# One computed order for all engines of a two-layer hybrid decoder trunk, with up products that keep tokens stationary and later transposes done by VectorE and DMAs

## The chip, the cores and the metric

The kernel runs on one core of one Trainium2 chip. The metric is the device time of one launch in microseconds (us); the figure used for a kernel is the median over its runs. Inside the core five engines run side by side: PE (TensorE, matmuls), DVE (VectorE), ACT (ScalarE), POOL (GpSimd) and SP (SyncE, which here only issues DMAs).

## What is computed

A trunk of two layers on 256 tokens of width 2048, all in float32. Layer 0 mixes tokens with a causal softmax attention of 16 heads and a forget gate ("fox"), layer 1 with three dilated window groups of 8 heads ("dil"). A squared-ReLU MLP of width 8192 follows each mixer.

```python
D_MODEL = 2048; SEQ = 256; DEPTH = 2; HEAD_DIM = 128; D_FF = 8192

def rms_norm(x, g):
    y = x * lax.rsqrt(jnp.mean(x * x, axis=-1, keepdims=True) + EPS)
    return y * g

def sq_relu_mlp(h, w_up, w_down):
    a = jax.nn.relu(h @ w_up)
    return (a * a) @ w_down

def reference(x, ...):
    for i in range(DEPTH):
        h = rms_norm(x, mix_norm_g[i])
        mix = fox_attention(h, ...) if i == 0 else dilated_attention(h, ...)
        x = x + mix                      # each mixer ends in o @ w_out
        h = rms_norm(x, mlp_norm_g[i])
        x = x + sq_relu_mlp(h, mlp_w_up[i], mlp_w_down[i])
    return x
```

In both attentions q and k are normed per head (`rms_norm(q, q_gain)`), and the mixers' input products are `h @ w_in`.

## The kernel before

**Products.** Float32 accuracy is had from fp32r matmuls: each operand is split into a high part (fp32r) and the rest, and a product is three matmuls, high*high + high*rest + rest*high. Weights come from HBM in pieces of 256 rows x 512 columns (`load`, L272, 512 KB, five buffers), and `split` cuts each on ACT (L288, `wh`, the high part) and DVE (L289, `wl`, the rest), five buffers each. A piece serves two steps k of 128 rows. `product` (L317 to L319) keeps the tokens of `hT` (or `aTh`/`aTl`, `oT`) as the stationary operand and streams 512 weight columns: for each k and each half of the tokens three matmuls of 512 columns into one PSUM bank. All mixers' input products, both output projections and the MLP's down products go this way.

**Up products.** `product_transposed` (L365, L369) keeps the weights stationary, so that the result comes out with channels on partitions, as the down product needs it. For each k and each of four blocks of 128 channels, one matmul streams the high and the rest parts of the 256 tokens side by side (512 columns, L365) and one streams the high part against the weights' rest (256 columns, L369). `up_chain` adds the two halves of each bank (ACT L842, DVE L843), squares (DVE L848) and splits (ACT L851, DVE L852) into `aTh` and `aTl`. The down product multiplies by the squared inverse norm at its end (`add_chain`, L805).

**Transposes.** Tokens with channels on partitions (`hT`) are made by `norm_chain`. For the first norm (`n0`) and for the last quarter of the three later ones PE transposes (L434, four 128x128 blocks at a time), since the next stage waits for these; the other quarters are turned by `transposed_by_dma`: DVE turns 32x32 blocks (L399), four DMAs write them to DRAM (L402), one reads them back (L404). Queries and keys go the same way in `qk_chain` (with the reading DMA on POOL's queue, L534), except two products (`by_engine`), which PE transposes (L506).

**Heads.** A head's work on PE is a group of score matmuls (L704, L610, L613), three transposes of the probabilities (`p_transposed`, L584) and the weighted values (`pv`, L576 and L577), with DVE and ACT between them.

**What sets the order.** The program writes instructions in one order and a scheduler places them; `Jobs` lets chains wait a fixed number of ticks (one tick is one k of a product) between their steps. `issue_after` holds some instructions behind others. Each engine runs its own instructions in order. At the start SP loads the first half of the first token block, half a weight piece (the other half goes by ACT's queue) and the second half of the block, and `wake` (L117) runs dummy transposes. `last_product` (L343 to L345) ends the kernel in three parts so that stores overlap.

Of the kernel before, what the change touches and what calls it, by code (L numbers as in the profile page):

```python
# [17 lines left out]
P = 128  # L18
# [5 lines left out]
KC = D // P  # L24
DFF = 4 * D
# [9 lines left out]
RAW_BUFS = 5  # L35
W_BUFS = 5
W_SUB = 2
RAW_SUB = 2


class Jobs:

    def __init__(self):
        self.now = 0
        self.live = []
        self.done = set()  # L50
        self.running = False

    def spawn(self, gen):
        self.live.append([self.now, None, gen])
        if not self.running:
            self._run()

    def _run(self):
        self.running = True
        for job in list(self.live):  # L60
            while job[0] <= self.now and (job[1] is None or job[1] in self.done):
                try:
                    got = next(job[2])
                except StopIteration:
                    self.live.remove(job)
                    break
                if isinstance(got, int):
                    job[0], job[1] = self.now + got, None
                    if not got:
                        continue  # L70
                else:
                    job[1] = got
        self.running = False

    def tick(self):
        self.now += 1
        self._run()

    def need(self, key):
        tries = 0  # L80
        while key not in self.done:
            self.tick()
            tries += 1
            assert tries < 10000, key
# [3 lines left out]
def trunk(ctx: ExitStack, tc, x, fox_w_in, fox_b_f, fox_q_gain, fox_k_gain, fox_w_out, dil_w_in,  # L88
          dil_q_gain, dil_k_gain, dil_w_out, mix_norm_g, mlp_norm_g, mlp_w_up, mlp_w_down, out):
    nc = tc.nc  # L90
    jobs = Jobs()

    const = ctx.enter_context(tc.tile_pool(name="const", bufs=1))
    act = ctx.enter_context(tc.tile_pool(name="act", bufs=1))
    wpool = ctx.enter_context(tc.tile_pool(name="wpool", bufs=1))
    work = ctx.enter_context(tc.tile_pool(name="work", bufs=1))
    small = ctx.enter_context(tc.tile_pool(name="small", bufs=8))
    dram = ctx.enter_context(tc.tile_pool(name="dram", bufs=1, space=bass.MemoryType.DRAM))
    ps_acc = ctx.enter_context(tc.tile_pool(name="ps_acc", bufs=4, space=PSUM))
    ps_tp = ctx.enter_context(tc.tile_pool(name="ps_tp", bufs=2, space=PSUM))  # L100
    ps_sc = ctx.enter_context(tc.tile_pool(name="ps_sc", bufs=2, space=PSUM))


    warm = small.tile([P, 1], F32, tag="warm", name="warm", bufs=1)
    nc.gpsimd.memset(warm, 0.0)
    nc.scalar.activation(warm, warm, AF.Exp)
    ident = const.tile([P, P], F32, name="ident")
    make_identity(nc, ident)
    mhalf = const.tile([P, 8], F32, name="mhalf")
    nc.gpsimd.memset(mhalf, -0.5)  # L110


    spare = ps_sc.tile([P, P], F32, tag="sc", name="spare")

    def wake(times):
        for _ in range(times):
            nc.tensor.transpose(spare, ident, ident)  # L117

    wake(8)


    gain = const.tile([P, 4 * KC + 8], F32, name="gain")
    MLP_G, FOX_G, DIL_G = 2 * KC, 4 * KC, 4 * KC + 2

    def gain_rows(name, sources):
        rows = work.tile([2 * KC, P], F32, tag="s", name=name, bufs=4)
        at = 0
        for src in sources:
            nc.sync.dma_start(rows[at:at + src.shape[0], :], src)
            at += src.shape[0]  # L130
        return rows[0:at, :]

    def gain_columns(name, rows, at):
        n = rows.shape[0]
        ps = ps_tp.tile([P, 512], F32, tag="tp", name=f"ps_{name}")
        nc.tensor.transpose(ps[:, :n], rows, ident[:n, :n])
        return nc.vector.tensor_copy(gain[:, at:at + n], ps[:, :n])

    per_chunk = "l (c p) -> (l c) p"
    mix_rows = gain_rows("g_mix", [mix_norm_g.rearrange(per_chunk, p=P)])  # L140


# [848 lines left out]
```

## Time and profile before

| What | us |
|---|---|
| median of 3 runs (lowest, highest) | 2164.76 (2164.07, 2165.49) |
| span of the profiled execution, first to last instruction | 2163.6 |
| PE busy | 2153.5 |
| DVE busy | 1395.5 |
| ACT busy | 1108.1 |
| POOL busy | 70.8 |
| DMA moved | 454.11 MB, 210 GB/s over the span |

The time of the profiled execution itself is not listed apart from its span; the median of the runs lies 1.2 us above that span. "Busy" of PE counts overlapping matmuls, so it says that PE has work, not how fast it goes; the pace is read from the distance between starts. Nearly the whole span PE is busy, at full granted clock in every slice, while DVE is busy for 64% and ACT for 51% of it.

### The profile page before, as it was taken

Reading aid. Unit: us, or ns where it says so; the run is one execution under the profiler, and the core shown is the slowest. Engines: PE = TensorE matmul, PEld = TensorE weight load, DVE = VectorE, ACT = ScalarE, POOL = GpSimd, SP = SyncE. Lnnn points to the kernel's source line nnn. Section 1 sums busy time; section 2 is a strip of 40 time slices with the busy share of each in tenths; the row PEclk is TensorE's granted clock in tenths of the full one; section 3 lists DMA queues with packets and bytes.
Section 4 is the critical chain, followed back from the end, with each engine's and each line's share of the span. In section 5 each row is a group of like instructions: output and inputs, shape, how many; then the busy total and the mean of one; then the engine's idle time right before and its main releaser. Section 6 shows DMA issues by size and latency. Waiting matters only on the chain.

```text
span 2163.6 us, 30020 instructions
## 1 busy us (share of the span) xinstructions
PE 2153.5 (100%) x11251; PEld 1918.3 (89%) x11251; DVE 1395.5 (64%) x1847; ACT 1108.1 (51%) x1536; POOL 70.8 (3%) x87
## 2 busy tenths in 40 slices
PE   9999999999999999999999999999999999999999
PEld 8888888998998998998888888888988988988988
DVE  6777796665665565566667777766655655655664
ACT  6655655544444454455555555655544543544542
POOL 1111000000000000000010010000000000000000
PEclk9999999999999999999999999999999999999999
DMA  8676658666666766767776776767666666666764
GB/s 253 219 224 190 222 175 264 200 202 202 201 203 203 200 201 204 203 199 242 216 251 204 242 224 198 240 203 237 203 204 201 199 204 204 200 202 203 203 211 140
DMA packets 285683, 454.11 MB, mean 210 GB/s; under 512 B 21144, under 2 KB 99040, under 8 KB 285536
## 3 DMA queue, kind: packets, MB, share of 16 engines
q1 hardware_dynamic: 282240, 442.36, 65.7%
q0 software_dynamic: 2880, 9.44, 1.2%
q8 instruction: 88, 1.44, 0.3%
q10 hardware_dynamic: 416, 0.39, 0.1%
q14 instruction: 59, 0.48, 0.1%
HBM read 435.86 MB, written 16.25 MB: 209 GB/s over the span
## 4 chain that ended last, share of the span: by engine, by line
PE 95%; DVE 2%; ACT 1%; DMA 1%; issue 1%; POOL 0%; SPq 0%; ACTq 0%; DVEq 0%; POOLq 0%
PE acc L318 20%; PE acc L319 20%; PE acc L317 20%; PE up_n3a_acc L365 5%; PE up_n1a_acc L365 5%; PE up_n3a_tp L365 3%; PE up_n3a_sc L365 3%; PE up_n1a_tp L365 3%; PE up_n1a_sc L365 3%; PE up_n1a_acc L369 3%; PE up_n3a_acc L369 3%; PE up_n1a_sc L369 1%; PE up_n3a_sc L369 1%; PE up_n1a_tp L369 1%; PE up_n3a_tp L369 1%; DVE wl L289 1%
## 5 line engine op out<-in xcount | busy, mean ns | idle before, releaser
L289 DVE TENSOR_TENSOR wl<-raw,wh 128x1024 fp32r<-128x1024 f32 x799 | 974.8, 1223 | 692.2 <-ACT wh L288 690.1
L288 ACT CAST wh<-raw 128x1024 fp32r<-128x1024 f32 x799 | 837.2, 1048 | 924.1 <-PE acc L319 591.7
L317 PE MATMUL acc<-wh,hT_n 128*128 128x512 f32 x896 | 344.4, 385 | 0.0
L318 PE MATMUL acc<-wl,hT_n 128*128 128x512 f32 x896 | 340.1, 380 | 0.1
L319 PE MATMUL acc<-wh,hT_n 128*128 128x512 f32 x896 | 340.0, 380 | 0.0
L317 PE MATMUL acc<-wh,aTh_n1a 128*128 128x512 f32 x512 | 194.0, 379 | 0.0
L318 PE MATMUL acc<-wl,aTh_n1a 128*128 128x512 f32 x512 | 194.0, 379 | 0.0
L319 PE MATMUL acc<-wh,aTl_n1a 128*128 128x512 f32 x512 | 194.0, 379 | 0.0
L319 PEld LDWEIGHTS acc<-wh,hT_n 128*128 128x128 f32 x896 | 169.6, 189 | 24.1
L317 PEld LDWEIGHTS acc<-wh,hT_n 128*128 128x128 f32 x896 | 170.0, 190 | 22.6 <-ACT hT_n L440 0.7
L318 PEld LDWEIGHTS acc<-wl,hT_n 128*128 128x128 f32 x896 | 169.9, 190 | 22.3 <-DVE wl L289 0.5
L317 PE MATMUL acc<-wh,aTh_n3a 128*128 128x512 f32 x480 | 181.9, 379 | 0.0
L318 PE MATMUL acc<-wl,aTh_n3a 128*128 128x512 f32 x480 | 181.9, 379 | 0.0
L319 PE MATMUL acc<-wh,aTl_n3a 128*128 128x512 f32 x480 | 181.9, 379 | 0.0
L365 PE MATMUL up_n1a_acc<-hT_n,wh 128*128 128x512 f32 x512 | 181.6, 382 | 0.0
L365 PE MATMUL up_n3a_acc<-hT_n,wh 128*128 128x512 f32 x512 | 181.6, 382 | 0.0
L369 PE MATMUL up_n1a_acc<-hT_n,wl 128*128 128x256 f32 x512 | 139.6, 273 | 0.0
L369 PE MATMUL up_n3a_acc<-hT_n,wl 128*128 128x256 f32 x512 | 139.6, 273 | 0.0
L318 PEld LDWEIGHTS acc<-wl,aTh_n1a 128*128 128x128 f32 x512 | 96.8, 189 | 13.8
L319 PEld LDWEIGHTS acc<-wh,aTl_n1a 128*128 128x128 f32 x512 | 96.8, 189 | 13.7
L317 PEld LDWEIGHTS acc<-wh,aTh_n1a 128*128 128x128 f32 x512 | 96.8, 189 | 13.6
L365 PEld LDWEIGHTS up_n1a_acc<-hT_n,wh 128*128 128x128 f32 x512 | 96.8, 189 | 13.5
(730 smaller groups left out, 3209.4 us busy)
## 6 DMA issues: line engine op xcount, KB each, us to landing
raw<-in_mlp_w_up_dram SPq DMA_DIRECT2D x256, 512.0 KB, 4.0
raw<-in_mlp_w_down_dram SPq DMA_DIRECT2D x256, 512.0 KB, 3.7
raw<-in_dil_w_in_dram SPq DMA_DIRECT2D x192, 256.0 KB, 3.2
raw<-in_fox_w_in_dram SPq DMA_DIRECT2D x95, 512.0 KB, 4.1
raw<-in_fox_w_out_dram SPq DMA_DIRECT2D x32, 512.0 KB, 3.9
raw<-in_dil_w_in_dram SPq DMA_DIRECT2D x32, 512.0 KB, 6.6
raw<-in_dil_w_out_dram SPq DMA_DIRECT2D x32, 512.0 KB, 4.5
blocks_n<-turned_n SPq DMA_DIRECT2D x72, 64.0 KB, 1.9
```

The source lines that it names most:

```text
L288: issued["cast"] = nc.scalar.copy(hi, raw)
L289: issued["cut"] = nc.vector.tensor_sub(lo, raw, hi.bitcast(F32))
L317: nc.tensor.matmul(acc[t], ah[:, tok], hi, start=first, stop=False)
L318: nc.tensor.matmul(acc[t], ah[:, tok], lo, start=False, stop=False)
L319: issued["product"] = nc.tensor.matmul(acc[t], al[:, tok], hi, start=False, stop=last)
L365: issued["product"] = nc.tensor.matmul(banks[b], hi[:, i, col], in_turn(tokens.rearrange("p x s -> p (x s)"), P // 2), start=first, stop=last)
L369: nc.tensor.matmul(banks[b][:, 0:S], lo[:, i, col], in_turn(tokens[:, 0, :], P // 2), start=False, stop=False)
```

## The change

The file is rewritten around a planner. The program no longer issues instructions as it goes; it records operations with an engine, a written-down duration, and the buffers they read and write. `Plan.order` then runs all of them once through a model of five engines (PE, ACT, DVE, POOL, DMA), takes on each engine the ready operation that is due first, and issues everything in the resulting order, with no scheduler behind it. What else is different:

- Up products use the same form as all others (`Unit.whole`, L384 to L386): tokens stationary, 512 weight columns streaming. From the second period of 2048 hidden columns on, blocks of an up unit alternate with blocks of a down unit of the period before (`UU_D`); a block is one weight piece, 12 matmuls.
- The result then has tokens on partitions. ACT takes the ReLU, scaled by the inverse norm (L952), DVE turns 32x32 blocks (L995), four DMAs write 128 KB each to DRAM and one reads 512 KB back (`through_dram`, L444, L449, all on SP's queue), ACT squares (L1003), and ACT and DVE split (L1008, L1010). The squared inverse norm in the down product's end is gone (L523 adds only).
- All transposes after the first norm go through DVE and DRAM, the last quarter of each norm (`normed`) and the two products that PE transposed included; POOL issues no DMA any more. PE keeps the transposes of the first norm and of the probabilities.
- Six buffers for weight pieces and four for each split part, with one more of each in the MLP phases (`MORE`).
- Two products that follow a norm are paired: six blocks of one, six of the other, then two and two (`paired`).
- The first two fox products (queries and keys) go two blocks at a time in turn.
- `HALVED` is empty, so `quarters` and `parts` never run; the token sums for them (`sums_of_tokens`, 8 times) are still made, and no product reads them.

The core of it:

```diff
+    def run(self):
+        engines = ("pe", "act", "dve", "pool", "dma")
...
+                heapq.heappush(rows[what.eng], (not what.urgent, what.due, what.i, what))
...
+            op = heapq.heappop(rows[eng])[-1]
+            op.at = now
...
+        def whole(self, raw, keys, j, first, last):
+            hi, lo = cut(raw, keys, 0, 2 * NC, j in self.adding)
+            for i in range(2):
+                k = 2 * j + i
+                def go(k=k, i=i):
+                    h, l = (in_turn(r(w)[:, i * NC:(i + 1) * NC], NC // 2) for w in (hi, lo))
+                    for t in range(NT):
+                        acc = v(self.banks[t])
+                        a, b = (self.source.at(k, x, t) for x in range(2))
+                        nc.tensor.matmul(acc, a, h, start=first and i == 0, stop=False)
+                        nc.tensor.matmul(acc, a, l, start=False, stop=False)
+                        nc.tensor.matmul(acc, b, h, start=False, stop=last and i == 1)
+                plan.product(6 * 0.216, go, [hi, lo, *self.source.keys(k)], self.banks)
-                def main(first, last):
-                    issued["product"] = nc.tensor.matmul(
-                        banks[b], hi[:, i, col], in_turn(tokens.rearrange("p x s -> p (x s)"), P // 2), start=first, stop=last)
-                def rest():
-                    nc.tensor.matmul(banks[b][:, 0:S], lo[:, i, col], in_turn(tokens[:, 0, :], P // 2), start=False, stop=False)
+    def through_dram(turned, into, size=NT * NC):
+        blocks = blocks_ring.take()
+        for i in range(4):
+            def go(i=i):
+                nc.sync.dma_start(v(blocks)[:, :, :, i, :].rearrange("t j c x -> c t j x"),
+                                  v(turned)[32 * i:32 * i + 32, 0:size].rearrange("p (t j x) -> p t j x", t=NT, j=4))
+            add("dma", 0.45, go, reads=[turned], writes=[(blocks, i)])
+        def back():
+            nc.sync.dma_start(v(into)[:, 0:size].rearrange("p (t y) -> p t y", t=NT),
+                              v(blocks).rearrange("t j c i x -> (j c) t (i x)"))
+        add("dma", moved(512), back, reads=[(blocks, i) for i in range(4)], writes=[into])
+    def up_end(l, phase, source, halved):
...
+                        nc.scalar.activation(halves(v(z)[:, t * NC:(t + 1) * NC], S), by_column(v(banks[t]), S), AF.Relu, scale=by(t))
...
+            add("dve", 1.4, lambda: nc.vector.transpose(
...
+            through_dram(turned, z)
...
+    UU_D = "UUDUDUDUDUDUDUDD"
...
+                for u, d in zip(ups, downs):
+                    for c in UU_D:
+                        (u if c == "U" else d).block()
...
+    def paired(a, b, n=6):
+        a.blocks(n)
+        b.blocks(n)
+        a.blocks(NP - n)
+        b.blocks(NP - n)
...
-    by_engine = {("fk", 3), ("dqk", 3, 2)}
-    def wake(times):
-    wake(8)
+    add("pe", 1.0, lambda: wake(8), writes=["woken"], urgent=True)
```

Three places of the order follow. The first is PE in an up product. Before (`up_n1a` are PSUM banks, `wl`/`wh` the parts of the weights, here two blocks of 128 channels and the start of the next product):

```order
L369 MATMUL up_n1a_0_acc_3865<-hT_n_7_3919,wl_3970 128x256
L365 MATMUL up_n1a_0_acc_3865<-hT_n_7_3919,wh_3969 128x512
L369 MATMUL up_n1a_0_acc_3866<-hT_n_7_3919,wl_3970 128x256
L365 MATMUL up_n1a_0_acc_3866<-hT_n_7_3919,wh_3969 128x512
L365 MATMUL up_n1a_1_tp_4124<-hT_n_0_3408,wh_4009 128x512 [waits Activation_49]
```

and now, where an up block (`bank_A`, tokens `hT`) ends and a down block (`bank_E`, `aT`) begins:

```order
L384 MATMUL bank_A<-hi_128,hT_112 128x512
L385 MATMUL bank_A<-lo_132,hT_112 128x512
L386 MATMUL bank_A<-hi_128,hT_112 128x512
L384 MATMUL bank_E<-hi_129,aT_116 128x512
L385 MATMUL bank_E<-lo_133,aT_116 128x512
L386 MATMUL bank_E<-hi_129,aT_116 128x512
```

Pairs of 512 and 256 columns became triples of 512, and down work stands between up blocks.

The second is PE at the start of the program. Before (`x_103` is the first token block, its halves on two DMA lanes):

```order
L117 MATMUL spare<-ident 128x128 [waits Pool_49]
L117 MATMUL spare<-ident 128x128 x7
L136 MATMUL ps_g_mix<-ident,g_mix 128x32 [waits DMAHW1_49]
L117 MATMUL spare<-ident 128x128 x3
L434 MATMUL ptx_n_0_146<-ident,x_103 128x128 [waits DMAHW2_49]
L434 MATMUL ptx_n_0_146<-ident,x_103 128x128 x3
L117 MATMUL spare<-ident 128x128 x3
L317 MATMUL acc_0_190<-wh_142,hT_n_0_151 128x512 [waits Activation_49]
```

and now:

```order
L655 MATMUL bank_C<-ident 128x128 [waits Pool_49]
L655 MATMUL bank_C<-ident 128x128 x7
L697 MATMUL bank_E<-ident,x_68 128x128 [waits DMAHW0_49]
L697 MATMUL bank_E<-ident,x_68 128x128 x3
L666 MATMUL bank_E<-ident,fox_s_163 128x32 [waits DMAHW2_49]
L697 MATMUL bank_E<-ident,x_68 128x128 [waits DMAHW4_49,DVE_49,Activation_49]
L697 MATMUL bank_E<-ident,x_68 128x128 x3
L384 MATMUL bank_A<-hi_126,hT_112 128x512
```

The transposes of the block's second half moved ahead of the first product, and the dummy transposes between are gone.

The third is ACT after an up product. Before (`up_chain`):

```order
L288 CAST wh_7267<-raw_7265 128x1024 [waits DMAHW7_49,DVE_49,PE_49]
L842 COPY z_n1a_2_0_7293<-up_n1a_2_sc_7108 128x256 [waits PE_49]
L842 COPY z_n1a_2_0_7293<-up_n1a_2_sc_7109 128x256 [waits PE_49]
L842 COPY z_n1a_2_1_7298<-up_n1a_2_acc_7110 128x256 [waits PE_49]
L288 CAST wh_7289<-raw_7287 128x1024 [waits DMAHW0_49,DVE_49,PE_49]
L842 COPY z_n1a_2_1_7298<-up_n1a_2_acc_7111 128x256
L851 CAST aTh_n1a_4_7304<-z_n1a_2_0_7293 128x512 [waits DVE_49]
```

and now (`up_end`; `mlp_z` holds the ReLU and then the rows read back from DRAM):

```order
L340 CAST mlp_hi_2630<-raw_123 128x1024 [waits DMAHW3_49,DVE_49,PE_49]
L952 ACTIVATE mlp_z_2627<-bank_A,rstd_75 128x512 [waits PE_49]
L952 ACTIVATE mlp_z_2627<-bank_A,rstd_75 128x512
L340 CAST hi_126<-raw_124 128x1024 [waits DMAHW4_49,DVE_49]
L340 CAST hi_127<-raw_125 128x1024 [waits DMAHW5_49,DVE_49,PE_49]
L340 CAST hi_128<-raw_120 128x1024 [waits DMAHW6_49,DVE_49,PE_49]
L340 CAST hi_129<-raw_121 128x1024 [waits DMAHW7_49,DVE_49,PE_49]
L340 CAST mlp_hi_2630<-mlp_raw_2629 128x1024 [waits DMAHW0_49,DVE_49,PE_49]
L1003 ACTIVATE mlp_tr_2624<-mlp_z_2627 128x4x128 [waits DMAHW4_49,DMAHW5_49,DMAHW3_49,DMAHW6_49,DMAHW1_49,DVE_49]
L1003 ACTIVATE mlp_tr_2624<-mlp_z_2627 128x4x128 [waits Activation_49]
L340 CAST hi_126<-raw_122 128x1024 [waits DVE_49,PE_49]
```

ACT now waits for a DMA in the middle of its casts, five casts after the ReLU; the casts that follow are queued behind that wait.

More of the change, by code (lines that the diff above doesn't have):

```diff
@@ L33 @@
 N_SLOPES = 3 * DH
[L35 to L84, printed above, removed]
+PERIODS = DFF // D
@@ L105, in trunk @@
+    warm = T["sm31"]
     nc.gpsimd.memset(warm, 0.0)
     nc.scalar.activation(warm, warm, AF.Exp)
[L107 removed]
     make_identity(nc, ident)
[L109 to L113 removed]
+    nc.gpsimd.memset(T["mhalf"], -0.5)
     def wake(times):
         for _ in range(times):
[L117 to L122 removed]
@@ L123, in trunk @@
[L123 to L137, printed above, removed]
+            nc.tensor.transpose(T["C1"][:, 0:P], ident, ident)
```

1669 lines of the change are left out of this document (957 added, 712 removed).

## The prediction

> **What bounds the kernel now.** I read the page of the profile first, then the waits of PE.
>
> ```profile
> span 2163.6 us, 30020 instructions
> ...
> PE 2153.5 (100%) x11251; PEld 1918.3 (89%) x11251; DVE 1395.5 (64%) x1847; ACT 1108.1 (51%) x1536; POOL 70.8 (3%) x87
> ...
> PE 95%; DVE 2%; ACT 1%; DMA 1%; issue 1%; POOL 0%; SPq 0%; ACTq 0%; DVEq 0%; POOLq 0%
> ```
>
> ```profile
> PE po_f L576 <- DVE pTl_f L589: 2.2, 3, 0.7
> ...
> PE pc L674 <- DVE g_lf L671: 1.1, 1, 1.1
> ...
> PE sc_d L610 <- DVE sd L759: 0.2, 1, 0.2
> ```
>
> PE is without work for 2163.6 - 2153.5 = 10.1 us, and only 2.2 + 1.1 + 0.2 = 3.5 us of that are waits inside the stream (columns: total, times, longest); the rest lies at the two ends. The chain of work that ended last is PE for 95%. So an edit is worth what it takes out of PE's stream or puts into it, and work on the other engines costs nothing until PE waits for it. The next view says how far they are from that (groups by line: busy, mean ns, idle before and whom it ended with).
>
> ```profile
> L289 DVE TENSOR_TENSOR wl<-raw,wh 128x1024 fp32r<-128x1024 f32 x799 | 974.8, 1223 | 692.2 <-ACT wh L288 690.1
> L288 ACT CAST wh<-raw 128x1024 fp32r<-128x1024 f32 x799 | 837.2, 1048 | 924.1 <-PE acc L319 591.7 <-PE up_n1a_acc L365 150.1 <-PE up_n3a_acc L365 150.0
> ```
>
> ACT's casts of weights stand idle 892 us (591.7 + 150.1 + 150.0) because PE has not yet freed a buffer: the cuts are ahead of PE, not behind it.
>
> **Pace of PE: -7.3 us.** Busy time says nothing of pace, since matmuls overlap; starts do. The timeline of PE gives the first and last of two unbroken stretches (start, length).
>
> ```profile
> 358.79 0.38 PE L317 MATMUL acc<-wh,oTfh 128*128 128x512 f32 x1
> ...
> 381.24 0.38 PE L319 MATMUL acc<-wh,oTfl 128*128 128x512 f32 x1
> ```
>
> ```profile
> 449.91 0.38 PE L365 MATMUL up_n1a_acc<-hT_n,wh 128*128 128x512 f32 x1
> ...
> 465.95 0.38 PE L365 MATMUL up_n1a_acc<-hT_n,wh 128*128 128x512 f32 x1
> ```
>
> The first is 105 matmuls with tokens stationary, so 22.45 / 104 = 0.2159 us from start to start. The second is 50 pairs of an up product, 16.04 / 49 = 0.3274 us for 512 + 256 columns. The new form streams the same columns as 1.5 matmuls of 512: 1.5 x 0.2159 = 0.3238. There are 2048 pairs (32 up products x 16 k x 4 blocks of channels), so 2048 x 0.0036 = 7.3 us go. I take this as certain to within 1 us: the form that replaces it is the one measured beside it, with the same weight loads.
>
> The Trainium skill (TensorE: Matmul & The Clock Gate, section Back-to-back issue gap) gives N/2.4 + 2.5 ns for a gap between matmuls. For 512 columns that is 215.8 ns, and the trace agrees. For 256 it is 109.2 ns, where the trace leaves 327.4 - 215.9 = 111.5. By the rule this term would be 2048 x 1.25 ns = 2.6 us and the time some 5 us higher; the trace decides.
>
> **Transposes taken from PE: -4.3 us.** Four in an up product, in the same timeline, and their counts by line:
>
> ```profile
> 383.86 0.38 PE L365 MATMUL up_n1a_acc<-hT_n,wh 128*128 128x512 f32 x1
> 384.07 0.60 PE L434 MATMUL ptx_n<-ident,x 128*128 128x128 f32 x4
> 384.43 0.36 PE L369 MATMUL up_n1a_sc<-hT_n,wl 128*128 128x256 f32 x1
> 384.62 0.38 PE L365 MATMUL up_n1a_sc<-hT_n,wh 128*128 128x512 f32 x1
> ```
>
> ```profile
> L434 PE MATMUL ptx_n<-ident,x 128*128 128x128 f32 x56 | 9.4, 295 | 0.3 <-DMA x<-in_x_dram 0.3
> ```
>
> From L365 to L365 it is 0.76 us where 0.33 is usual: 0.43 for four. The code leaves 32 of the 56 (the first norm) and takes 24, and all 16 of L506: ten groups, 4.3 us. A late turn through DRAM could give some of it back; paired units put 12 blocks, 12 x 12 x 0.2159 = 31.1 us, ahead of the first product that needs the last quarter, and the turn has a price in the trace:
>
> ```profile
> L399 DVE STREAM_TRANSPOSE turned_n<-x 128x512 f32<-128x512 f32 x18 | 12.6, 700 | 0.0
> L842 ACT COPY z_n1a<-up_n1a_acc 128x256 f32<-128x256 f32 x32 | 11.8, 369 | 0.0
> L843 DVE TENSOR_TENSOR z_n1a<-up_n1a_acc,z_n1a 128x256 f32<-128x256 f32 x32 | 13.2, 414 | 0.0
> L848 DVE SCALAR_TENSOR_TENSOR z_n1a<-z_n1a 128x512 f32<-128x512 f32 x32 | 21.8, 680 | 0.0
> L851 ACT CAST aTh_n1a<-z_n1a 128x512 fp32r<-128x512 f32 x32 | 19.9, 623 | 4.4 <-DVE z_n1a L848 4.4
> ```
>
> ```profile
> raw<-in_mlp_w_up_dram SPq DMA_DIRECT2D x256, 512.0 KB, 4.0
> ...
> blocks_n<-turned_n SPq DMA_DIRECT2D x72, 64.0 KB, 1.9
> ```
>
> Turning 1024 columns is 2 x 0.70 on DVE, four writes that land in 1.9 us at half the new size (taken twice, 3.8), a read of 512 KB (4.0, as a weight piece) and a cast and a cut of 1.05 and 1.22: 11.5 us, some 15 with scaling and queues. That fits into 31.1 twice.
>
> **The up rows' new road: nothing.** Per up unit ACT had four L842 and two L851 (2.7 us) and now has two ReLUs and two squares (four of about 0.62, as L851) and a cast of 1.05: 3.5. DVE had four L843, two L848 and two of L852 like it (4.4) and now 1.40 + 1.22 = 2.6. With 16 pieces of 1.05 and 1.22 in the 41.4 us of an up and a down unit (32 steps of six matmuls), ACT comes to some 20 of 41.4 and DVE to 22. The road takes about 14 us by the same rows, 18 with queues; the blocks behind which its product stands are 13 in the interleaved periods, 33.7 us. ACT's wait for the read-back has five casts ahead of it, and what is queued behind it are casts, for which PE would wait only after it has used up those five, 5 x 2.59 = 13 us. If the cover were gone, each us of delay would be a us of the kernel. The token sums that nothing reads (8 times about 4 us on two engines) stay under the same cover.
>
> DMA: 32 x 1 MB more.
>
> ```profile
> 550.00:600.00 50.00, 50.00 (x308) 46.04 (x307) 30.67 (x36) 25.06 (x32) 0.00 (x0) 1.00 0.68 201
> ```
>
> The engines' share is 0.68 (before the GB/s). By bytes (1 MB on 8) it becomes 0.77; if each 512-byte packet cost as much as one of 2 KB, 1280 packets on 4096 make it 0.89. Neither bounds. On SP the writes and the read stand between weight loads that are six or seven pieces ahead.
>
> **Waits in the stream: -2.0 us.** The 3.5 us may vanish or grow. Before, the weighted values stand 12 products behind their transposes in 15 of 16 fox heads, and three of these waited 0.7 us. In the new order 12 of 16 stand 18 to 48 products behind, the dil heads 18 to 42, and the four at 12 have a score group between. Scores stand 138 products (29.8 us) or more behind their key unit; the same chain before:
>
> ```profile
> 130.50 0.69 ACT L484 ACTIVATE sq_('fk', 1)_0_1427<-acc,rstd_n 128x512 f32<-128x512 f32 x1
> ...
> 156.08 0.42 DVE L552 TENSOR_TENSOR fkT_1l<-sq_('fk', 1)_0_1427,fkT_1h 128x256 fp32r<-128x256 f32 x1
> ```
>
> 26 us. So I leave 1.5 us of waits. Bounds: none, or 0.7 at each of the 32 weighted products, 22.4 us.
>
> **Start: +1.0 us.** PE's first rows, and the stretches of the first 10 us (last two columns: DMA share, GB/s):
>
> ```profile
> 5.30 1.12 PE L434 MATMUL ptx_n<-ident,x 128*128 128x128 f32 x4 [0.32 <-DMA x<-in_x_dram]
> 6.21 0.85 PE L117 MATMUL spare<-ident 128*128 128x128 f32 x3
> 6.98 0.80 PE L317 MATMUL acc<-wh,hT_n 128*128 128x512 f32 x1
> ...
> 9.27 0.63 PE L319 MATMUL acc<-wh,hT_n 128*128 128x512 f32 x1
> 9.70 1.06 PE L434 MATMUL ptx_n<-ident,x 128*128 128x128 f32 x4
> 10.41 1.10 PE L317 MATMUL acc<-wh,hT_n 128*128 128x512 f32 x2
> ```
>
> ```profile
> 2.00:4.00 2.00, 2.00 (x9) 1.67 (x9) 0.43 (x1) 0.75 (x2) 1.84 (x4) 1.00 0.87 225
> 4.00:6.00 2.00, 1.68 (x8) 1.21 (x9) 0.94 (x9) 0.62 (x1) 0.50 (x2) 1.00 0.93 306
> ...
> 8.00:10.00 2.00, 2.00 (x7) 1.53 (x6) 1.16 (x2) 0.46 (x1) 0.00 (x0) 1.00 0.97 324
> ```
>
> Now the first product stands behind the second half of the token block, the fifth transfer on SP: 256 + 512 + 16 + 512 + 256 KB = 1.59 MB. At those rates 0.45 + 0.61 MB are in by 6.0, and the rest at 324 GB/s by 7.6. Four transposes take 0.91 there (5.30 to 6.21), so the first product starts near 8.6 instead of 6.98, 1.6 later, with a transpose group done that stood at 9.70 and took 0.71. Net 0.9, rounded to 1.0. The slow products at the beginning, 2.29 us for the five steps to 9.27, or 0.46 apart, come in both: PE has little to do before them either way. Bounds: -1 (the later token blocks need no waiting) to +5 (they land late, as the weights for two units now share the DMA with them).
>
> The Trainium skill (TensorE: Matmul & The Clock Gate, section What's actually happening) says that PE starts at half clock and leaves it after about 3.4 us of sustained work, in windows that do not start with the kernel. The trace fits (0.46 apart here, 0.2159 later), though its granted clock shows 1.00 there. By the rule, with no dummy transposes in between, PE would be at half clock for 3.4 us after 7.6 and lose 1.7 us; the trace before lost about as much, so the term stays.
>
> **Sum.** 2163.6 - 7.3 - 4.3 - 2.0 + 1.0 = 2151.0 us of span. The median of the runs shown lies 1.2 above the span: 2152.2, so 2152.
>
> **Rivals.**
> - *Slower: PE waits at the heads.* The planner works with written durations; if its heads come late, PE stands at a fixed place in the order with ready products behind it. For it: the three waits of 0.7 above are of this kind. Against: the distances grew. At 0.7 for each of 32 weighted products 20.9 us are added to the sum, 2173. It decides from 18 us of such waits on (2152.2 + 16.9 = 2169.1).
> - *The start is starved.* x blocks two to four come behind weight pieces of two units, and PE waits for them ahead of its products: +4, 2156. For it: DMA shares of 0.87 to 0.97 in the rows above; against: the pieces in front are needed anyway.
> - *The pace of up products doesn't change.* If the 256-column matmuls were not what costs the 0.0036, only transposes and waits go: 2152.2 + 7.3 = 2159.5. Against: two stretches within 110 us of each other, both without a gap. (The Trainium skill's formula above stands between: 2157.)
> - *No wait is left and the start is even.* 2163.6 - 7.3 - 4.3 - 3.5 + 1.2 = 2149.7.
>
> **How the numbers follow.** My forecast has 0.48, no wait left 0.22, starved start 0.14, unchanged pace 0.06, waits at the heads 0.10. Within 0.2% of 2164.8 (about what a measurement here can tell from no change) is 2160.4 to 2169.1. The first three cases are below it, and half of the fourth; the other half and half of the fifth lie within; what is left of the fifth is slower, and I move 0.03 there from faster for what no row shows: faster 0.84, same 0.08, slower 0.08. The range goes from 2147 (no wait and a start that gains) to 2160, above which only the heads' case lies.
>
> **What would show it.** In the new profile: up products (L384 to L386 on `hT` in the MLP) 0.216 apart, 22 us per 104 without a gap; no PE transposes but L697 and L623; the waits of PE on DVE and ACT below 3 us after the first 60 us; the first product at 8 to 9 us; weight casts on ACT still idle for PE and not the other way. It is wrong if PE shows several hundred waits for `hi` or `lo` in the MLP phases (cuts late behind ACT's wait for the read-back), if the score or weighted groups each wait most of a us, or if PE's pace over a block exceeds 2.59 us.

## The result and the profile after

The changed kernel takes 2153.57 us (median of 4 runs, 2153.05 to 2153.84) where the kernel before takes 2164.66 beside it: a ratio of 0.9948, 95% interval 0.9934 to 0.9962. Its profiled execution has a span of 2151.5 us and a time of 2153.44. The forecast was 2152, with 2151.0 for the span.

The page of the changed kernel, the rows that answer to those of before (the last two are groups by line: busy, mean ns, idle before and whom it ended with):

```profile
span 2151.5 us, 27374 instructions
...
PE 2138.8 (99%) x10181; PEld 1877.5 (87%) x10181; DVE 1357.0 (63%) x1492; ACT 1124.2 (52%) x1424; POOL 57.3 (3%) x51
...
PE 99%; DMA 0%; DVE 0%; ACT 0%; issue 0%; SPq 0%; ACTq 0%
...
L346 DVE TENSOR_TENSOR lo<-raw,hi 128x1024 fp32r<-128x1024 f32 x638 | 778.8, 1222 | 505.4 <-ACT hi L340 485.9
L340 ACT CAST hi<-raw 128x1024 fp32r<-128x1024 f32 x638 | 667.6, 1047 | 645.1 <-PE bank_A L386 258.0
```

PE is still the chain, now for 99% of it, and 1070 matmuls shorter. ACT's casts of weights still stand idle for PE (the row names the largest of the releasers alone) and PE for no cast: none is in the waits of PE below.

Where the 12.1 us of span went is read from four marks in the timeline of PE: the first product of the first MLP, of the third stage, of the second MLP, and the last matmul. Before:

```profile
381.45 0.38 PE L365 MATMUL up_n1a_sc<-hT_n,wh 128*128 128x512 f32 x1
...
1049.21 0.38 PE L317 MATMUL acc<-wh,hT_n 128*128 128x512 f32 x1
...
1491.19 0.38 PE L365 MATMUL up_n3a_sc<-hT_n,wh 128*128 128x512 f32 x1
...
2159.20 0.28 PE L345 MATMUL last<-wh,aTl_n3a 128*128 128x256 f32 x1
```

After (the bracket is the idle time ahead of the row and who ended it):

```profile
378.70 0.46 PE L384 MATMUL bank_A<-mlp_hi,hT 128*128 128x512 f32 x1 [1.36 <-issue]
...
1043.38 0.46 PE L384 MATMUL bank_B<-hi,hT 128*128 128x512 f32 x1 [1.40 <-DVE x L523]
...
1483.59 0.38 PE L384 MATMUL bank_A<-mlp_hi,hT 128*128 128x512 f32 x1
...
2147.92 0.28 PE L1194 MATMUL bank_A<-mlp_hi,aT 128*128 128x256 f32 x1
```

| stage | before, us | after, us | difference |
|---|---|---|---|
| first stage (fox), from the span's start | 381.45 | 378.70 | -2.75 |
| first MLP | 667.76 | 664.68 | -3.08 |
| third stage (dil) | 441.98 | 440.21 | -1.77 |
| second MLP | 668.01 | 664.33 | -3.68 |
| from the last matmul to the end | 4.40 | 3.58 | -0.82 |

Two of the marks carry a wait of 1.4 us that the forecast did not have. All waits of PE in the changed kernel (total, times, longest):

```profile
PE bank_E L697 <- DMA x<-in_x_dram: 2.7, 2, 2.5
PE bank_C L655 <- POOL ident masks.py:199: 1.7, 1, 1.7
PE bank_B L384 <- DVE x L523: 1.4, 1, 1.4
PE bank_A L384 <- issue: 1.4, 1, 1.4
PE bank_E L666 <- DMA fox_s<-in_mix_norm_g_dram: 1.0, 1, 1.0
PE bank_B L1192 <- DVE x L1207: 0.8, 1, 0.8
PE bank_A L384 <- ACT aT L642: 0.5, 1, 0.5
```

Three of them (L697, L655, L666) lie in the first 9 us. Of the other 4.1 us none is at a score or a transpose of the heads; three stand where one unit's banks are read while the next unit wants to write them, at the turns of stages and in the last unit. The fourth (0.5) is a last head's row arriving at its output projection.

### The profile page after: what moved, and what is told of

It is laid out like the page before. It is cut to its first block, busy times and chain, and to the rows that moved or that the text cites. A ratio compares the mean times of both kernels' runs of the same rounds, so it can differ in the third digit from the quotient of the medians.

```text
span 2151.5 us, 27374 instructions
## 1 busy us (share of the span) xinstructions
PE 2138.8 (99%) x10181; PEld 1877.5 (87%) x10181; DVE 1357.0 (63%) x1492; ACT 1124.2 (52%) x1424; POOL 57.3 (3%) x51
## 4 chain that ended last, share of the span: by engine, by line
PE 99%; DMA 0%; DVE 0%; ACT 0%; issue 0%; SPq 0%; ACTq 0%
PE bank_A L384 15%; PE bank_A L386 14%; PE bank_A L385 14%; PE bank_B L384 11%; PE bank_B L386 11%; PE bank_B L385 11%; PE bank_E L386 6%; PE bank_E L385 6%; PE bank_E L384 6%; PE bank_C L611 1%; PE bank_C L639 0%; PE bank_C L609 0%; PE bank_E L623 0%; PE bank_C L640 0%; DMA x<-in_x_dram 0%; PE bank_B L1192 0%
## 5 line engine op out<-in xcount | busy, mean ns | idle before, releaser
L346 DVE TENSOR_TENSOR lo<-raw,hi 128x1024 fp32r<-128x1024 f32 x638 | 778.8, 1222 | 505.4 <-ACT hi L340 485.9
L340 ACT CAST hi<-raw 128x1024 fp32r<-128x1024 f32 x638 | 667.6, 1047 | 645.1 <-PE bank_A L386 258.0
L384 PE MATMUL bank_A<-hi,hT 128*128 128x512 f32 x1136 | 432.9, 381 | 0.0
L386 PE MATMUL bank_A<-hi,hT 128*128 128x512 f32 x1136 | 431.4, 380 | 0.0
L385 PE MATMUL bank_A<-lo,hT 128*128 128x512 f32 x1136 | 431.3, 380 | 0.0
L386 PEld LDWEIGHTS bank_A<-hi,hT 128*128 128x128 f32 x1136 | 215.1, 189 | 31.0 <-DVE hT L707 0.5
L384 PEld LDWEIGHTS bank_A<-hi,hT 128*128 128x128 f32 x1136 | 215.4, 190 | 29.7
L385 PEld LDWEIGHTS bank_A<-lo,hT 128*128 128x128 f32 x1136 | 215.3, 189 | 29.8
L384 PE MATMUL bank_B<-hi,hT 128*128 128x512 f32 x512 | 196.2, 383 | 1.4 <-DVE x L523 1.4
L385 PE MATMUL bank_B<-lo,hT 128*128 128x512 f32 x512 | 194.1, 379 | 0.0
L386 PE MATMUL bank_B<-hi,hT 128*128 128x512 f32 x512 | 194.1, 379 | 0.0
L384 PE MATMUL bank_B<-hi,aT 128*128 128x512 f32 x504 | 191.5, 380 | 0.0
L386 PE MATMUL bank_B<-hi,aT 128*128 128x512 f32 x504 | 191.0, 379 | 0.0
L386 PE MATMUL bank_E<-hi,aT 128*128 128x512 f32 x416 | 157.7, 379 | 0.0
L384 PE MATMUL bank_E<-hi,aT 128*128 128x512 f32 x416 | 157.7, 379 | 0.0
L384 PEld LDWEIGHTS bank_B<-hi,hT 128*128 128x128 f32 x512 | 96.8, 189 | 14.5 <-issue 1.8
L386 PEld LDWEIGHTS bank_B<-hi,hT 128*128 128x128 f32 x512 | 96.8, 189 | 13.7
```

The source lines that it names most:

```text
L340: add("act", on_act(n), lambda: nc.scalar.copy(r(hi)[:, 0:n], v(src)[:, at:at + n]), reads=keys, writes=[hi])
L346: add("dve", on_dve(n), lambda: nc.vector.tensor_sub(r(lo)[:, 0:n], v(src)[:, at:at + n], v(hi)[:, 0:n]), reads=[*keys, hi], writes=[lo])
L384: nc.tensor.matmul(acc, a, h, start=first and i == 0, stop=False)
L385: nc.tensor.matmul(acc, a, l, start=False, stop=False)
L386: nc.tensor.matmul(acc, b, h, start=False, stop=last and i == 1)
```

## The experiments

All but the last two edit the changed kernel, 2153.6; those two edit the version of 2149.0 ahead of them. Each was timed beside the kernel before, whose medians were 2164.86 to 2164.89.

**The pace: short matmuls put back.** In the up products:

```diff
-nc.tensor.matmul(acc, b, h, start=False, stop=last and i == 1)
+for y in range(2):
+    n = slice(y * P, (y + 1) * P)
+    nc.tensor.matmul(acc[:, y * S:(y + 1) * S], b, h[:, :, n, :], start=False, stop=last and i + y == 2)
```

> The changed kernel, but in the up products of both MLPs the third matmul of each three (token remainder times rounded weights, 512 columns) is issued as two of 256 columns with the same stationary tile. That puts 2048 matmuls of 256 columns back into PE's stream, as many as the kernel before had, and the columns streamed stay the same. My theory (the short matmuls were what cost the 0.0036 us per pair): 2048 x 0.0036 = +7.3 us over the changed kernel's 2153.6, so 2160.9, with an up product's group of four matmuls 2 x 0.2159 + 2 x 0.1115 = 0.655 us apart instead of 0.648. Rival 1, the Trainium skill's formula N/2.4 + 2.5 ns (TensorE: Matmul & The Clock Gate, section Back-to-back issue gap): 2048 x 0.00125 = +2.6 us, 2156.2. Rival 2, the pace came from the operands' roles (which one is stationary) and not from the length: no change, 2153.6.

Measured: 2161.66 (2160.17 to 2163.78), ratio 0.9985 [0.9976, 0.9994], so +8.1. Its timeline, the first of 31 groups of four matmuls without a gap and the start of the down block behind the last of them:

```profile
448.02 0.38 PE L385 MATMUL bank_B<-hi,hT 128*128 128x512 f32 x1
...
468.32 0.38 PE L385 MATMUL bank_E<-hi,aT 128*128 128x512 f32 x1
```

20.30 / 31 = 0.6548 us for a group, 0.0071 more than three matmuls at 0.2159, so 1024 x 0.0071 = 7.3 (the median has 0.8 more, within the spread of its runs). Operands and columns are the same as in the changed kernel; what differs is the length, and with it the number of matmuls and of weight loads, one for each matmul (1024 more of both). That rules out both rivals: the short matmuls, each with its load, cost what the forecast took off. Which of the two costs it is not separated.

**The transposes: 102 groups put back.**

```diff
+if turn:
+    for b in range(4):
+        nc.tensor.transpose(T["C1"][:, 0:P], ident, ident)
 h, l = (in_turn(r(w)[:, i * NC:(i + 1) * NC], NC // 2) for w in (hi, lo))
```

> The changed kernel with 102 groups of four 128-column transposes of the identity put back into PE's stream, one group ahead of every fifth up step of the two MLPs; nothing reads what they write. My theory (a group costs what the trace of before shows between two up products, 0.43 us, wherever it stands): 102 x 0.43 = +43.9 us over 2153.6, so 2197.5, and ten groups are 4.3 us. Rival: part of the 0.43 was the change between kinds of matmul and is hidden or larger here: a group at 4 x 0.0555 (a quarter of a 512-column matmul each) would give +22.6, 2176; one with a drained pipeline at 0.6 would give +61, 2215.

Measured: 2198.99 (2197.81 to 2202.77), +45.4, or 0.445 a group. One of them in its timeline:

```profile
453.25 0.38 PE L395 MATMUL bank_B<-hi,hT 128*128 128x512 f32 x1
453.46 0.60 PE L388 MATMUL bank_C<-ident 128*128 128x128 f32 x4
453.82 0.46 PE L393 MATMUL bank_B<-hi,hT 128*128 128x512 f32 x1
454.12 0.38 PE L394 MATMUL bank_B<-lo,hT 128*128 128x512 f32 x1
```

From 453.25 to 454.12 it is 0.87 where two matmuls take 0.43: 0.44 for the group, 0.08 of it in the product behind it. Ten groups are 4.4 us. The price rests on the median and on this row, not on the profiled span: that execution was the slowest of the five, and at the start of the third stage it waits 3.79 us where the changed kernel waits 1.40.

**The waits at the turns of stages: other banks.**

```diff
-banks = AC if halved else ("A0", "A1") if b or n % 2 == 0 else ("B0", "B1")
+banks = AC if halved else ("A0", "A1") if b else (("B0", "B1"), ("A0", "A1"), ("E0", "E1"), ("B0", "B1"))[n]
...
+next_banks()
 oD = Source()
```

> The changed kernel with other banks for the accumulators at two places: the four up units of an MLP's first period take B, A, E, B instead of A, B, A, B, and the units of the third stage (dil) start one place further in the turn of A and B. So the unit that begins a stage no longer writes the pair of banks that the unit before has just finished. My theory (the 1.36 us at 377.3 and the 1.40 us at 1042.0 are PE waiting for the addition of the finished pair to x on VectorE): both go, 2.8 us less, 2150.8 of median and waits of PE on x L523 gone. Rival 1: what PE waits for at the stage's begin is its weights or token rows (cuts into buffers of the new stage), the bank only ends at the same time: then the wait stays, 2153.6. Rival 2: the stall moves to a later unit, because the banks come round again: 2153.6 with another row of the waits at 1 us or more.

Measured: 2150.42 (2149.9 to 2150.8), ratio 0.9933 [0.992, 0.9945], so -3.1. Both rows of 1.4 are gone from its waits (2.8 us in all) and none took their place. The row that the profile put down to "issue" was the same wait: VectorE's addition to x ran from 377.38 to 378.60 there, on bank A.

**The start, both halves of the first block in front.**

```diff
-add("dma", moved(256), go, writes=[("x0", "half", part)])
+add("dma", moved(256), go, writes=[("x0", "half", part)], urgent=True)
```

> The changed kernel with both halves of the first token block issued as the first two transfers on SP, ahead of the weights; everything else as the planner then orders it. My theory (the first product stands behind the transposes of the second half, which landed at 8.7 as fifth transfer): first product at 7.0 to 7.9 instead of 9.49, when the first weight piece is in (768 KB in front of it at 225 to 281 GB/s from 1.9 on, and 1.05 for its cast), so 1.6 to 2.5 us less, about 2151.7. Rival 1: the weights of the second unit come later by as much and PE waits there instead: 2153.6, with a wait for a cast within the first 15 us. Rival 2: PE's slow first rows (0.43 apart until 13.5) last a fixed time from the first product, so the gain is whole, 2 us; if they end at a fixed point of the timeline, half of the gain goes: 2152.6.

Measured: 2155.36 (2154.78 to 2157.16), ratio 0.9958 [0.9945, 0.997]: 1.8 slower than the changed kernel. The theory did not hold. The first product came at 9.20, 0.3 earlier, since now the gain rows were late, and a score group stood ahead of its keys, which no head does in the changed kernel. The first product of the third unit, where the stream is even again, stands at 62.44 instead of 61.38, and the score group waits 1.3 us more behind that. Rows of its waits:

```profile
PE bank_E L666 <- DMA fox_s<-in_mix_norm_g_dram: 2.0, 1, 2.0
...
PE bank_C L611 <- DVE fox_kl L589: 0.9, 1, 0.9
...
PE bank_C L611 <- ACT fox_kh L588: 0.4, 1, 0.4
```

**The unused token sums left out.** `begin_norm(..., False)` at both MLPs.

> The changed kernel without the token sums of the two MLP norms: eight times four additions and one subtraction of 256 to 1024 columns on VectorE and one cast on ScalarE, whose results nothing reads. My theory (they lie under PE's stream): no change, 2153.6 within 0.7. Rival: they delay the additions to x and the norms at the turn of a stage, where PE waits; then up to 1 us at each MLP's begin goes, 2151.6.

Measured: 2153.82 (2153.36 to 2154.9). No change: they lie under the cover of PE's stream.

**The cover of the up rows' road halved.**

```diff
-UU_D = "UUDUDUDUDUDUDUDD"
+UU_D = "DDDDDDDDUUUUUUUU"
```

> The changed kernel with another interleave of up and down units in the periods that hold both: eight blocks of the down unit, then eight of the up unit (before: two up, then in turn, then two down). The work is the same; what changes is what stands between the end of a period's last up unit and the first product that reads its rows: six down blocks, 6 x 2.59 = 15.5 us, instead of thirteen, 33.7 us. In the changed kernel's trace the road runs from the first ReLU at 539.6 to the squares' end at 553.7; with the cast and the cut behind it (1.05 + 1.22) and the last product's end ahead it is 16.5 us. My theory (the road is hidden by that cover alone, and each us beyond it is a us of the kernel): about 1 us of PE waiting on aT at each of the six turns, +6, 2159.6, and at most +15 if the road takes 18 us under the denser traffic. Rival 1: the road is much shorter when it is urgent, as the planner then puts its casts first: no change, 2153.6. Rival 2: the road is not what the order protects; eight up pieces in a row starve PE of cuts instead: waits for hi or lo, +20 or more.

Measured: 2169.28 (11 runs, 2165.91 to 2171.8), ratio 1.0019 [1.001, 1.0028], so +15.7. Its profiled execution was the fastest of the eleven (span 2163.9, +12.4); the waits for up rows in it:

```profile
PE bank_E L386 <- DVE aT L1010: 4.5, 6, 0.8
PE bank_E L384 <- ACT aT L1008: 3.3, 5, 1.0
```

7.8 us at six turns, 1.3 a turn. So the road is 16.8 us there (15.5 + 1.3), it is hidden by the blocks between, and no cast was short. But the span grew by more than the waits. The timeline behind the first of them:

```profile
477.73 0.48 PE L384 MATMUL bank_E<-hi,aT 128*128 128x512 f32 x1 [0.99 <-ACT aT L1008]
...
479.18 0.48 PE L386 MATMUL bank_E<-hi,aT 128*128 128x512 f32 x1 [0.75 <-DVE aT L1010]
...
480.26 0.63 PE L384 MATMUL bank_E<-hi,aT 128*128 128x512 f32 x1
480.69 0.63 PE L385 MATMUL bank_E<-lo,aT 128*128 128x512 f32 x1
...
483.56 0.38 PE L386 MATMUL bank_E<-hi,aT 128*128 128x512 f32 x1
```

From 480.26 to 483.25 matmuls start 0.43 us apart, seven of them at twice the price: 1.5 us on top of the 1.7 of waits. A stretch of it (its length, busy time of PE, PEld, DVE, ACT and POOL, the granted clock, DMA share, GB/s):

```profile
470.00:477.00 7.00, 6.74 (x32) 5.57 (x30) 2.69 (x3) 3.46 (x6) 0.00 (x0) 1.00 0.98 346
477.00:484.00 7.00, 5.52 (x17) 4.25 (x18) 3.26 (x3) 2.56 (x3) 0.00 (x0) 0.76 0.50 169
```

The clock granted falls to 0.76 there. Only one of the six turns shows it in this execution, the one with the longest waits; four others hold pairs of waits as close together (0.42 to 0.68 and then about 0.75) and keep the clock at 1.00. That the runs which took up to 6 us longer had more such stretches is not shown, since only this one was profiled. What is left of the 12.4 over 7.8 + 1.5 are restarts of 0.1 to 0.2 us behind each wait and rows below a tenth, not separated.

**The start again, gains second.** The gains' transfer made urgent, and the second half's transposes planned 5 us later.

```diff
-writes=[pt], urgent=True, late=0.3)
+writes=[pt], urgent=True, late=5.0 if n == 0 and pr == 1 else 0.3)
```

> The changed kernel with two edits at the start: the 16 KB of norm gains are issued on SP second, behind the first half of the first token block, and the transposes of the second half are given a later planned time, so that they stand behind the first weight piece's first twelve products and their transfer third in front of the second weight piece. In the run with both halves in front the first product came at 9.20 for 9.49, held by the gain rows, which landed at 7.16, and 2.9 us were lost by the end of the first stage. My theory (the first product needs only the first half, the gains and the first weight piece): first product at 6.7 to 7.3, 2 to 2.7 us earlier than 9.49, and 1.5 to 2.5 us less in all, about 2151.5. Rival 1: what is won is lost to the second weight piece, which lands no earlier than before (the bytes ahead of it are the same): PE waits 1 to 2 us there, 2153.6. Rival 2: the moved order of casts makes a score group of the first heads wait, as in the run with both halves in front (0.9 and 0.4 us there, and 1.5 us more in rows without a named wait): 2154 to 2156.

Measured: 2156.53 (2156.21 to 2158.46), slower again by 3. The gains were ready at 5.46, but their use stands behind the first weight cast on ScalarE, and that weight piece landed at 7.75 instead of 5.78 (5.95 us behind its issue instead of 4.48). The likely cause is the half block, which was issued right behind it (0.46 us) and was on the way at the same time; this was not tried apart. The first product came at 9.22, a little earlier, but the third unit's at 64.00 instead of 61.38: nearly all of the loss lies in the first stage's start.

**Everything together, with that start.** For the last unit `("B0", "A0", "C0")` instead of `("B0", "B1", "A0")`.

> The start of the run before this one, the other banks at the beginnings of stages, and for the last down unit's three parts accumulators in three separate tiles (B, A and C instead of two halves of B, and A). My theory (the parts add up: 3.1 measured for the banks, 2 for the start, 0.8 for the wait on the last unit's first addition): 2153.6 - 5.9 = 2147.7, with PE's first matmul of the second part of the last unit no longer behind the addition of the first. Rival: the wait of 0.78 in the last unit is not one for the neighbouring half of a bank pair but the drain of PE itself: then 2148.5 and the row stays. If the start brings nothing: 2149.7.

Measured: 2152.16 (2151.42 to 2153.02), ratio 0.994 [0.9928, 0.9953]. The parts did not add up, since the start lost what it lost alone; the wait in the last unit was gone.

**The banks and the last unit, with the changed kernel's own start.**

> The changed kernel with its own start, the other banks at the beginnings of stages, and accumulators in three separate tiles (B, A, C) for the last down unit's three parts. My theory (the additions to x are what PE waits for at 377.3, 1042.0 and 2142.2, and each wait ends when no unit writes the pair of banks that is being read): 2153.6 - 3.1 (measured with the banks alone) - 0.8 = 2149.7, with no wait of PE over 0.6 us behind the first 60 us. Rival: the tail's last transfer ends the execution whatever PE does before it (it is issued 0.45 us behind the last addition, and the first two parts' transfers are in front): then the banks alone count, 2150.4.

Measured: 2149.01 (2148.47 to 2149.38), ratio 0.9925 [0.9912, 0.9939], 4.6 us less than the changed kernel and the fastest version of all. All its waits of PE:

```profile
PE bank_E L697 <- DMA x<-in_x_dram: 3.4, 2, 3.1
PE bank_C L655 <- POOL ident masks.py:199: 1.7, 1, 1.7
PE bank_E L666 <- DMA fox_s<-in_mix_norm_g_dram: 1.0, 1, 1.0
PE bank_B L384 <- ACT aT L642: 0.5, 1, 0.5
```

Behind the start one wait of 0.5 us is left in 2147.2 us. The three waits that went come to 3.5 of the 4.6; what the rest is was not separated. The 0.8 in the last unit was thus a wait for the addition that reads the other half of the same tile: with three tiles it goes.

**Dummy transposes ahead of the first product.** `wake(8)` behind the gains' transpose.

> The run before this one with eight transposes of the identity on PE directly behind the transpose of the norm gains (at 5.99 there), in the stretch in which PE waits for the second half of the first token block (until 8.75). Nothing reads them. In the changed kernel the first products run 0.43 us apart from 10.06 to 13.2 and 0.2159 from 13.58, nine of them at + 0.21. My theory (PE is at half clock as long as it has not been busy for some 3.5 us, so work ahead of the first product counts): full rate from about 10.5 instead of 13.4, 5 to 7 products at half the price, 1.1 to 1.5 us less: 2148.4. Rival 1: the rate rises at a time that the first product sets, whatever ran before: 2149.7, unchanged. Rival 2: the weights' second piece or its cut is then the bound (the next casts come 2.2 us apart): half of it, 2149.1, with a wait for lo or hi in the first 15 us.

Measured: 2148.74 (2147.58 to 2150.14), which cannot be told from 2149.01. In its profiled execution, its slowest, the first product was at 10.28 and the rate rose at 15.21, no sooner than without them (12.68 there). Undecided for the median, nothing in the trace for it.

**The first product ahead of the second half's transposes.**

```diff
 q_unit.blocks(2)
+turned_at[0, 1].before.add(plan.products[1])
```

> The first run of these three with one more edge for the planner: the transposes of the second half of the first token block stand behind the first twelve products (which need the first half alone) instead of ahead of them. The transfers keep their order. My theory (the first product stands at 9.49 only because it is queued behind those transposes): first product at 7.2 to 7.6, and some 1 us less in all, since the thirteenth product then waits for the second half's scaling, which ScalarE has behind five weight casts: 2148.7. Rival 1: that wait takes all of it: 2149.7. Rival 2: the work that the planner moves behind it makes a score group of the first heads wait, as in both other starts tried: 2151 or more.

Measured: 2153.99 (2152.23 to 2154.81), 5 slower than the same kernel without the edge. The first product came at 7.18, 3.1 us earlier, and more than that was lost behind it. Rows of its waits:

```profile
PE bank_A L386 <- DVE hT L709: 1.6, 1, 1.6
PE bank_E L698 <- ACT hT L706: 1.4, 1, 1.4
...
PE bank_C L611 <- DVE fox_kl L589: 0.5, 1, 0.5
```

PE waits for scaled token rows (L706, L709) that stand behind weight casts on ScalarE: the first of them runs at 13.49, right behind three casts. The third unit's first product comes at 63.94, where it is 61.33 without the edge. So the first product's time is not what the start is worth.

## Why the prediction was right, point by point

| term | forecast | measured | from |
|---|---|---|---|
| pace of the up products | -7.3 | -7.2 | both MLPs, below |
| ten groups of transposes | -4.3 | -4.4 | 10 x 0.44, groups put back |
| waits in the stream | -2.0 | +0.6 | 3.5 before, 4.1 after |
| start | +1.0 | +1.6 | third unit's first product, below |
| behind the last matmul | 0 | -0.8 | marks |
| nothing of the forecast | 0 | -1.9 | remainder of -12.1, below |

**Pace.** The MLPs took 3.08 and 3.68 less; without the waits of 1.40 and 0.78 in them it is 4.48 and 4.46. Two groups of transposes stood in each (0.88), so 3.6 each, 7.2 in all. The new pace is as forecast, the first and last of 105 matmuls through up and down blocks:

```profile
543.02 0.38 PE L386 MATMUL bank_B<-hi,aT 128*128 128x512 f32 x1
...
565.47 0.38 PE L385 MATMUL bank_E<-lo,aT 128*128 128x512 f32 x1
```

22.45 / 104 = 0.2159. The Trainium skill's formula (TensorE: Matmul & The Clock Gate, section Back-to-back issue gap), which that section gives for a single isolated matmul and which would have made this term 2.6, is not borne out for 256 columns beside 512: the run with short matmuls paid 0.0036 for each, not 0.0013.

**Transposes.** Right, and the group's price holds at places where nothing was turned before.

**Waits: the step that failed.** "So I leave 1.5 us of waits" looked for them at the heads alone. There it was more than right: not one is left, and the slower rival (0.7 at each weighted product) did not come. But the new kernel holds accumulators in pairs of banks, each pair one tile, and one addition of 1.22 us reads a whole pair. Where the turn of A and B makes the next unit take the pair just finished, PE waits for that addition: 1.36, 1.40, and 0.78 in the last unit. The bank names stand in the order's rows; the forecast did not follow them across the turns. The runs with other banks showed it: these waits went, and 4.6 us of the median with them. How long such a wait is depends on what VectorE has in front of the addition: in the run with 102 groups a cut of token rows and a cut of weights ran ahead of it while PE stood, and the wait of 1.40 became 3.79.

**Start.** The landing was misjudged, and with it perhaps the size. The second half landed later than 7.6, and the first product came at 9.49 instead of 8.6. Rows of the changed kernel:

```profile
8.75 1.08 PE L697 MATMUL bank_E<-ident,x 128*128 128x128 f32 x4 [2.46 <-DMA x<-in_x_dram]
9.49 0.77 PE L384 MATMUL bank_A<-hi,hT 128*128 128x512 f32 x1
...
13.58 0.38 PE L384 MATMUL bank_A<-hi,hT 128*128 128x512 f32 x1
```

What it cost in the end is read at the third unit's first product, before and after:

```profile
60.26 0.36 PE L674 MATMUL pc<-g_lf,tri 128*128 128x16 f32 x2 [1.10 <-DVE g_lf L671]
...
60.92 0.46 PE L317 MATMUL acc<-wh,hT_n 128*128 128x512 f32 x1
```

```profile
61.38 0.38 PE L384 MATMUL bank_E<-hi,hT 128*128 128x512 f32 x1
```

It is 0.46 later though the wait of 1.10 ahead of it is gone: some 1.6, not 1.0. In the six other profiled executions with this start left as it is (short matmuls, groups, both runs with other banks, no token sums, half the cover) this product stands at 60.76 to 61.85, so the 1.6 may be anything from 1.0 to 2.1, and the forecast of 1.0 lies at its edge. The rival of a starved start (x blocks two to four late) did not come: two waits for x are in the list, both for the first block. The edits that moved the start all lost.

**The up rows' road.** Hidden, as said: no wait of PE on it. In the changed kernel it takes from 539.56 (first ReLU) to 553.70 (squares) and a cast and a cut, within the 14 to 18 given. The DMA share was forecast at 0.77 by bytes, 0.89 by packets:

```profile
550.00:600.00 50.00, 50.00 (x233) 43.79 (x232) 25.55 (x22) 24.16 (x27) 0.00 (x0) 1.00 0.76 236
```

It is 0.76. One sentence was too kind: with the cover gone "each us of delay would be a us of the kernel". In the run with half the cover 7.8 us of waits cost 12.4, and in the median 15.7.

**What cancelled.** Waits and start came out 3.2 us worse than forecast, and 2.7 came back that no term had. Of these 0.8 lie behind the last matmul: the last store's transfer, from its issue to the end of the span, takes 3.57 us in the profile of before and 2.79 to 2.91 in every profile of the new kernel and its variants; why is open. The other 1.9 lie in the two attention stages, where the first is 1.5 and the third 0.3 shorter than their groups, waits and start explain. The timeline has most of the 1.5. Before, 11 of the 16 score groups of the fox heads stand right behind transposes of probabilities, and there the group's first matmul (L704) takes 0.25 us to the next start:

```profile
105.31 0.49 PE L584 MATMUL ptp_f<-ident,s_f 128*128 128x128 f32 x3
105.55 0.41 PE L704 MATMUL sc_f<-negc,sel 128*128 128x384 f32 x1
105.80 0.38 PE L610 MATMUL sc_f<-fkT_1w,fqT_1w 128*128 128x128 f32 x2
```

Now all 16 stand behind a product, and the same matmul (L849) takes 0.16:

```profile
96.35 0.33 PE L849 MATMUL bank_C<-fox_negc,fox_sel 128*128 128x384 f32 x1
96.51 0.39 PE L609 MATMUL bank_C<-fox_kw,fox_qw 128*128 128x128 f32 x2
```

That is 11 x 0.085 = 0.9 us. Behind each of the three waits of 0.7 that went, the weighted product's matmuls (L576) also stood 0.26 us further apart than without a wait, 0.8 in all. These are readings of one profile each, and no run tried them apart. So the total is right by more than its terms are, and that part is luck.

## What to carry to other kernels

When PE is the bound, price a matmul by its start-to-start distance in unbroken stretches, form by form; two forms of the same columns can differ by a per cent, and the estimate held to 0.1 us in 7. When accumulators are handed round, follow the bank names across every turn of a stage, since a unit that takes the pair just finished waits for its whole read; giving it another pair was worth 4.6 us here, while every attempt on the order of the start lost. And don't value a start by its first product: follow it to a point where the stream is even.

## What the runs showed of the hardware

PE's clock can fall in the middle of a dense stream, and these runs do not settle what sets it off. Behind waits of 0.99 and 0.75 within 1.5 us of each other PE ran seven matmuls at 0.43 (clock 0.76 over that stretch, above). Slightly shorter pairs in the same execution were not followed by this, nor were the waits of 1.42, 1.62 and 0.68 between 12.5 and 18.6 us in the last run, where the clock stays at 1.00. In the run with 102 groups seven slow matmuls follow a single wait of 3.79, which ends at 1068.53:

```profile
1068.00:1073.00 5.00, 4.47 (x13) 3.70 (x14) 1.96 (x4) 1.45 (x4) 0.70 (x1) 0.66 0.81 206
```

No single wait of up to 2.23 us in the stream (the longest, in the run without token sums, ends at 379.29) was followed by slow matmuls in any trace here. The Trainium skill (TensorE: Matmul & The Clock Gate, section What's actually happening) has PE fall back to half rate after an idle window of about 3.4 us. The wait of 3.79 agrees; the two short ones come to 1.74 with work between them, so that rule does not account for them, and their case stays open.

From the first product to the full rate it took 4.1 us in the changed kernel (9.49 to 13.58), 2.4 in the same start with other banks (10.27 to 12.68), and 4.9 with dummy transposes in front (10.28 to 15.21). So a first product that is 0.8 later can lose nothing, and differences of a us at the start mean little in one execution.

Two halves of one accumulator tile were not independent in this program: PE waited 0.78 us to write one half while VectorE read the other, and with separate tiles it did not. Whether the chip needs that wait, or only the program's own dependencies asked for it, no run separates.
